# Delta rule of a hybrid layer: inverses' copies on ScalarE, fillers ahead of the first inverse, the third group's masks by adding transfers

## The chip, the cores and the metric

One core of a Trainium2 chip. The time is that of the device, in microseconds (us), from one launch; it is given as the median of several runs. Beside it stands one execution that the hardware profiler took. The engines are TensorE (PE: matmuls; PEld: its weight loads), VectorE (DVE), ScalarE (ACT), GpSimd (POOL) and SyncE (SP), which here only issues transfers. Each engine works off its own queue in order.

## The reference

One layer over 512 latent tokens and 256 context tokens, width 1024: half-step SwiGLU, then neighbourhood attention and a bidirectional gated delta rule (4 heads of 128) side by side, merged by sigmoid gates, then a second SwiGLU. The change is in the delta rule and at one place of the second SwiGLU. The delta rule in chunks, for keys k, values v, log decay g (summed inside the chunk) and beta:

```
decay = exp(where(lower, g[..., :, None] - g[..., None, :], -inf))
m     = where(strict, (k * beta) @ k.T * decay, 0)
u, w  = solve(I + m, [v * beta, k * beta * exp(g)])     # unit lower triangular
step:   v_new = u - w @ s
        o     = (q * exp(g)) @ s + (q @ k.T * decay) @ v_new
        s     = s * exp(g_last) + (k * exp(g_last - g)).T @ v_new
```

It runs forward and backward in time, first over the context, then over the latent tokens with the state that the context left.

## The kernel before, in words

All matmuls are in f32 split into a high and a low part (`split`, L137 on ACT and L139 on DVE), three products for one. Weights come through a stream (`Stream`): a transfer to `wr` (L175), a cast to `wh`, a difference `wl`. A weight can be queued behind instructions named in `behind`: the cast on ACT behind the first, the difference on DVE behind the second. For the second SwiGLU that table is `ws.behind` (L1654); `norms[t]` holds, for token tile t, the instruction that makes the normalized y (L130 on ACT) and the one that makes its bias nb (L129 on DVE).

The delta rule works on chunks of 128 tokens. There are six steps s = 0 to 5, in three groups of two (`bi` = 0, 1, 2), which makes four scans in a group, and for each step two pairs of heads p, each with two directions: four 128x128 matrices per (p, s).

`gram(p, s)` makes the decay matrix Dt and the two products. SP broadcasts a row of summed decays to all partitions (L1124); four DVE instructions subtract the partition's own sum and add the mask (L1128); ACT takes the exponential (L1129). Then Bt = products x beta x Dt (L1134, DVE), which goes out to DRAM (`bd`, L1137), and At for the outputs (L1140). `decay_place` says which buffer Dt has: the two buffers of tag `Dt` for s=0 and 1 with p=0 and for s=3, 4 and 5, parts of the output accumulators `oacc` for the rest.

`base_inverse` loads the 32x32 diagonal blocks of one group (L1158) into L, sets L's diagonal on POOL (L1161), and inverts them by 31 rows on DVE, each a product `bt` (L1165) and a sum `Xt` (L1166). It is a generator that stops after every fourth row. The result goes to DRAM (`rd`, L1169). L has one buffer, so a group's blocks can only be loaded when the rows of the group before are done.

`inverse` puts the blocks together to 128x128 inverses, two of them per group. It loads blocks (T<-rd, L1186), transposes them on DVE (L1188, L1189), copies them to T6 (L1199, ACT) and Tt (L1200, POOL), and then goes to and fro: small matmuls into `pi`, a copy Y to SBUF (L1208, DVE, 128x128), matmuls, negated copies (L1224 DVE, L1225 ACT), matmuls, a copy Y6 (L1235, DVE, 128x256; the profile writes Y for both), matmuls, a last negated copy into Tt (L1243, ACT).

`scan_step` is the recurrence: state times keys, `r` (L1266, DVE), inverse times r, `vn` (L1275, DVE), the scaled keys `ktail` (L1280, ACT), the new state (L1290, DVE), and for s >= 2 the outputs. After the last scan `gdn_out` normalizes them.

PE has few matmuls here and long waits between them, so other work is put between: the projections `FILLS`, 28 weight tiles of 8 k-slices, in quarters. One quarter (here: one step) is two slices with three 128x512 matmuls each. `turn(kind, i)` is called behind each group of small matmuls; it adds a rate from `RATE` to `due`, and issues as many whole steps as are due, behind the last matmul. Kind g stands in the products, l once before the first inverse, i in the inverses, s in the scans. Behind the last scan a loop (L1410) issues steps until all but the last `NLATE` tiles are done and a tile is complete; what is left follows with attention.

The order on each engine is made by a planner from program order and its own clock; `tc.issue_after(x)` forces an instruction behind x on the same engine. `marks` keeps the instructions for that. The program order of the delta rule is at its end: `grams` of a group, then `inv_of` (the inverses) and `scan_of`, with `step(base, n)` running n pieces of the base inverse of the group to come.

Of the kernel before, what the change touches and what calls it, by code (L numbers as in the profile page):

```python
# [12 lines left out]
AF = mybir.ActivationFunctionType  # L13
ALU = mybir.AluOpType
# [4 lines left out]
P = 128  # L19
# [39 lines left out]
def body(ctx, tc, I, out, dbg=None):  # L59
# [986 lines left out]
    spool, done = [gq], [0]  # L1046
    gb_, close_gb = pool("gbase", "right")
    FS, N0, NKQ, NLATE = 4, 2, 2, 3
    RATE = {"g": (2, 3.0, 0.7), "l": (7.2,), "i": (1.5, 0, 0), "s": (0.7, 0.9, 0.5)}
    NBT, NAT, NT6, NTT = 8, 8, 1, 2  # L1050

    last = [None]

# [59 lines left out]
    def decay_place(s, p):  # L1113

        if s == 2 or s < 2 and p == 1:
            a = 2 * (s == 2)
            return oaccs[p if s == 2 else s][:, a:a + 2].rearrange("p a b c -> p (a b) c")
        return tl(gb_, [P, 4, P], "Dt", 2)[:]

    def gram(p, s, bd, g):  # L1120

        mats = mats_of(s)
        Dt = decay_place(s, p)
        nc.sync.dma_start(Dt[:], bass.AP(gcd.tensor, gcd.offset + (4 * s + 2 * p) * P, [[0, P], [24 * P, 2], [1, 2 * P]]))  # L1124
        for m, (d, c, i) in enumerate(mats):
            msk = cst[:, (C_MF if d == 0 else C_MB):][:, 0:P]
            with tc.issue_after(marks["At" if s > 3 else "Bt"]) if s > 1 else nullcontext():
                V.scalar_tensor_tensor(Dt[:, m], Dt[:, m], gcum[:, d, s, 2 * p + i:2 * p + i + 1], msk, op0=ALU.subtract, op1=ALU.add)  # L1128
        S.activation(Dt[:], Dt[:], AF.Exp)  # L1129
        Bt, At = tl(gq, [P, 4, P], "Bt", NBT), None  # L1130
        for n, t in enumerate(products(p, s)):
            if n == 0:
                for m, (d, c, i) in enumerate(mats):
                    b = V.scalar_tensor_tensor(Bt[:, m], t[m] if s == 1 else t[:, m], beta[:, d, s, 2 * p + i:2 * p + i + 1], Dt[:, m], op0=ALU.mult, op1=ALU.mult)  # L1134
                if s < 2:
                    marks["Bt"] = b.ins
                nc.sync.dma_start(bass.AP(bd.tensor, bd.offset + g * MSTR, [[P, P], [4 * MSTR, 4], [1, P]]), Bt[:])  # L1137
            else:
                At = tl(gq, [P, 4, P], "At", NAT)
                a = V.tensor_tensor(At[:], t[:], Dt[:], ALU.mult)  # L1140
                if s < 4:
                    marks["At"] = a.ins
        return Bt, At


    def base_inverse(bd, rd):


        L = tl(gb_, [P, 32, 32], "L")
# [12 lines left out]
        for i in range(1, 32):  # L1162
            c = (i + 1) // 2
            t = tl(gb_, [P, 16, 32], "bt")
            V.tensor_tensor(t[:, 0:c, 0:i + 1], L[:, i:i + 1, 0:i + 1].to_broadcast([P, c, i + 1]), Xt[:, 0:c, 0:i + 1], ALU.mult)  # L1165
            V.tensor_reduce(Xt[:, 0:c, i], t[:, 0:c, 0:i + 1], AX, ALU.add, negate=True)  # L1166
            if i % 4 == 0:
                yield
# [10 lines left out]
    def inverse(bi, st, rd, Bts):  # L1179
# [16 lines left out]
        bt = lambda k, b: Bts[k % 2][:, k // 2 + (0 if b else 2)]  # L1196
        for b, r in enumerate(blk):
            o = 32 * (b % 2)
            S.copy(T6[r, :, o:o + 32], T0[r])  # L1199
            G.tensor_copy(Tt[r, :, 32 * b:32 * b + 32], T1[r])  # L1200
        py = tl(pgq, [P, 4, 32], "pi", 2)
        for k in range(4):
            for b, r in enumerate(blk):
# [1 line left out]
                mm(py[r, k, :], bt(k, b % 2)[q, r], T0[q, m, :], start=True, stop=True, tile_position=(32 * (b ^ 1), 32 * b))  # L1205
        turn("i", bi)
        Y = tl(gq, [P, 4, 32], "Y2", 2)
        V.tensor_copy(Y[:], py[:])  # L1208
        p0 = tl(pgq, [P, 4, 32], "pi", 2)
        p1 = tl(pgq, [P, 4, 32], "pi", 2)  # L1210
        for k in range(4):
# [20 lines left out]
                mm(py[hb[b], k, :], bt(k, b)[hb[1 - b], hb[b]], T6[hb[1 - b], m, :], start=True, stop=True, tile_position=(64 * (1 - b), 64 * b))  # L1232
        turn("i", bi)
        Y6 = tl(gq, [P, 4, 64], "Y6")
        V.tensor_copy(Y6[:], py[:])  # L1235
        p1 = tl(pgq, [P, 4, 64], "pi", 2)
        for k in range(4):
            for b in range(2):
# [1 line left out]
                mm(p1[hb[1 - b], k, :], Y6[hb[b], k, :], Tt[hb[b], m, hb[b]], start=True, stop=True, tile_position=(64 * b, 64 * (1 - b)))  # L1240
        turn("i", bi)
        for b in range(2):
            S.activation(Tt[hb[1 - b], sysm(b), hb[b]], p1[hb[1 - b]], AF.Copy, scale=-1.0)  # L1243
        return [[Tt[:, 4 * d + 2 * i + p] for d in range(2) for i in range(2)] for p in range(2)]

    def bc4(t, s, p):

        return t[:, :, s, 2 * p:2 * p + 2, None].to_broadcast([P, 2, 2, P])

    def v4(t):  # L1250
        return t.rearrange("p (d i) c -> p d i c", d=2)
# [3 lines left out]
    def scan_step(p, s, Tt, At, Sst):  # L1255
# [19 lines left out]
        V.tensor_tensor(v4(vn[:]), v4(pv[:]), bc4(beta, s, p), ALU.mult)  # L1275
# [57 lines left out]
    def grams(bi):  # L1333
        bd = tl(dp, [16 * MSTR], f"bd{bi}")[:]
        rds[bi] = tl(dp, [64, 1024], f"rd{bi}")[:]
        for j in (0, 2, 1, 3) if bi == 0 else range(4):
            res[(bi, j)] = gram(j % 2, 2 * bi + j // 2, bd, 2 * (j % 2) + j // 2)
        return base_inverse(bd, rds[bi])

    def step(gen, n=8):  # L1340
        for _ in range(n):
# [309 lines left out]
    ws = Stream(wp, [(w, key(j)) if key(j) else w for j, w in enumerate(src)], WB, 2)  # L1651
    ws.extra = {"b": (wb, 4, wp, WB), "c": (wc, 2, wp, WB)}

    ws.behind = {j: (norms[t]["y"], norms[u][m]) for j, t, u, m in ((2, 1, 2, "nb"), (3, 1, 2, "nb"), (4, 2, 3, "x2"), (5, 2, 3, "x2"), (6, 2, 3, "nb"), (7, 2, 3, "nb"))}  # L1654

    def h2(p, n):
        hs.append((tl(p, [P, NX], "hh", n, F32R), tl(p, [P, NX], "hl", n, F32R)))
# [280 lines left out]
```

## Time and profile before

| what | value |
|---|---|
| median of 3 runs | 1485.09 us (1483.22 to 1487.64) |
| the profiled execution's own time | 1482.26 us |
| its span, first to last instruction | 1480.5 us |
| mean granted TensorE clock | 0.995 of full speed |
| VectorE busy in the whole span | 77% |

How to read it: a page of the profile gives each engine's busy time; a list of waits names who waited for whom, with total, number and longest wait; a timeline row has the start in us, the duration, engine, line, operation, out<-in, shapes and count, and in brackets the idle time of the engine before it and what ended it; a row of a stretch gives its length, then for each engine the busy time and the number of instructions (PE, PEld, DVE, ACT, POOL), the granted clock, the share of the DMA engines and GB/s; a row of a group has its busy time, the mean of one in ns, and the idle time before.

### The profile page before, as it was taken

How to read it: one execution, taken by the hardware profiler on the slowest of the kernel's cores; microseconds unless marked ns; L12 is line 12 of the kernel's file. 1: busy time of each engine (PE TensorE's matmuls, PEld its weight loads, DVE VectorE, ACT ScalarE, POOL GpSimd, SP SyncE). 2: the span in 40 equal slices, each digit the busy share in tenths (PEclk: the TensorE clock that was granted, in tenths of full speed). 3: DMA queues.
4: the chain of work that ended last, by engine and by line, in shares of the span. 5: the costliest groups of instructions: out<-in, count | busy, mean ns of one | idle time of the engine just before them, and what ended most of it. 6: DMA issues, size and time to landing. Idle time of an engine off the chain costs nothing.

```text
span 1480.5 us, 23912 instructions
## 1 busy us (share of the span) xinstructions
PE 1430.8 (97%) x9117; PEld 1255.9 (85%) x9117; DVE 1144.0 (77%) x1975; ACT 661.7 (45%) x1090; POOL 214.6 (14%) x262
## 2 busy tenths in 40 slices
PE   6999999999999999999999899999999999999997
PEld 4789889999997777888877778877788999998886
DVE  8688869999987666768787885676668799886627
ACT  5435523434333387545544434376426454444310
POOL 1000000000000111223201001352321022220001
PEclk9999999999999999999999999999999999999999
DMA  9677764444569444222476523283344133234722
GB/s 377 206 250 250 240 232 172 162 161 165 164 212 400 181 160 150 79 93 94 153 227 209 163 68 126 93 302 108 120 157 171 38 129 114 94 106 144 257 99 85
DMA packets 109236, 248.56 MB, mean 168 GB/s; under 512 B 29049, under 2 KB 44481, under 8 KB 109121
## 3 DMA queue, kind: packets, MB, share of 16 engines
q1 hardware_dynamic: 104480, 229.40, 45.8%
q0 software_dynamic: 3056, 12.33, 2.2%
q10 hardware_dynamic: 1586, 5.32, 0.9%
q8 instruction: 71, 1.16, 0.3%
q14 instruction: 43, 0.35, 0.1%
HBM read 215.50 MB, written 31.50 MB: 167 GB/s over the span
## 4 chain that ended last, share of the span: by engine, by line
PE 72%; DVE 11%; DMA 8%; issue 3%; ACT 3%; POOL 2%; SPq 1%; DVEq 0%; POOLq 0%; ACTq 0%
PE ps L212 17%; PE ps L534 5%; PE ps L536 5%; PE ps L535 5%; PE pm L193 4%; PE pm L194 4%; PE pm L195 4%; PE ps L193 3%; PE ps L195 3%; PE ps L194 3%; PE ps L1712 3%; PE ps L1714 3%; PE ps L1713 3%; PE pc L1055 2%; DVE wl L139 2%
## 5 line engine op out<-in xcount | busy, mean ns | idle before, releaser
L137 ACT CAST wh<-wr 128x1024 fp32r<-128x1024 f32 (+1 forms) x184 | 185.4, 1013 | 270.6 <-PE pm L194 67.5
L139 DVE TENSOR_TENSOR wl<-wr,wh 128x1024 fp32r<-128x1024 f32 (+1 forms) x184 | 225.1, 1228 | 102.2 <-ACT wh L137 101.8
L193 PE MATMUL pm<-uxh,wh 128*128 128x512 f32 x320 | 131.3, 410 | 0.2
L195 PE MATMUL pm<-uxh,wl 128*128 128x512 f32 x320 | 126.3, 395 | 1.0 <-DVE wl L139 1.0
L194 PE MATMUL pm<-uxl,wh 128*128 128x512 f32 x320 | 126.0, 394 | 0.0
L212 PE MATMUL ps<-wh,hx 128*128 128x512 f32 x352 | 96.3, 391 | 1.1 <-ACT wh L137 1.1
L212 PEld LDWEIGHTS ps<-wh,hx 128*128 128x128 f32 x352 | 65.9, 188 | 15.7 <-ACT wh L137 1.9
L281 DVE SCALAR_TENSOR_TENSOR adap<-wr,crow 128x1024 f32<-128x1024 f32 x61 | 74.3, 1218 | 0.7 <-ACT crow L289 0.3
L195 PEld LDWEIGHTS pm<-uxh,wl 128*128 128x128 f32 x320 | 60.5, 189 | 14.2 <-DVE wl L139 1.2
L114 POOL TENSOR_TENSOR rs<-ve,mhalf 128x1 f32<-128x1 f32 (+2 forms) x46 | 50.3, 1095 | 141.5 <-DVE ve L110 139.1
L193 PEld LDWEIGHTS pm<-uxh,wh 128*128 128x128 f32 x320 | 60.7, 190 | 11.3 <-ACT u L152 0.4
L194 PEld LDWEIGHTS pm<-uxl,wh 128*128 128x128 f32 x320 | 60.7, 190 | 10.4
L193 PE MATMUL ps<-uh,wh 128*128 128x256 f32 (+1 forms) x208 | 68.2, 328 | 0.4 <-ACT wh L137 0.4
L194 PE MATMUL ps<-ul,wh 128*128 128x256 f32 (+1 forms) x208 | 67.3, 324 | 0.0
L195 PE MATMUL ps<-uh,wl 128*128 128x256 f32 (+1 forms) x208 | 67.1, 325 | 0.0
L194 PE MATMUL ps<-uxl,wh 128*128 128x256 f32 (+1 forms) x192 | 60.5, 317 | 0.8 <-DVE uxl L139 0.8
L137 ACT CAST wh<-ra 128x1024 fp32r<-128x1024 f32 x31 | 32.6, 1052 | 62.1 <-PE ps L535 20.2
L195 PE MATMUL ps<-uxh,wl 128*128 128x256 f32 (+1 forms) x192 | 60.2, 317 | 0.0
L193 PE MATMUL ps<-uxh,wh 128*128 128x256 f32 (+1 forms) x192 | 59.7, 317 | 0.0
L534 PE MATMUL ps<-ur,wh 128*128 128x384 f32 x168 | 56.5, 336 | 0.0
L535 PE MATMUL ps<-ur,wh 128*128 128x384 f32 x168 | 56.4, 336 | 0.0
L534 PE MATMUL ps<-uh,wh 128*128 128x384 f32 x168 | 56.4, 336 | 0.0
(502 smaller groups left out, 4246.8 us busy)
## 6 DMA issues: line engine op xcount, KB each, us to landing
wr<-in_w_adaT_dram SPq DMA_DIRECT2D x64, 512.0 KB, 4.6
wr<-in_up_dram SPq DMA_DIRECT2D x56, 512.0 KB, 3.4
wr<-in_win_dram SPq DMA_DIRECT2D x52, 512.0 KB, 3.4
wr<-in_dn_dram SPq DMA_DIRECT2D x51, 512.0 KB, 3.7
ra<-in_up_dram SPq DMA_DIRECT2D x24, 512.0 KB, 4.3
rb<-in_up_dram SPq DMA_DIRECT2D x18, 512.0 KB, 3.3
ra<-in_w_adaT_dram SPq DMA_DIRECT2D x16, 512.0 KB, 4.5
wr<-in_w_o_dram SPq DMA_DIRECT2D x8, 512.0 KB, 4.3
```

The lines of the kernel that those rows point to most:

```text
L114: G.tensor_tensor(rs[:], ve[:], mhalf[:, 0:n], ALU.pow)
L137: marks["hi"] = S.copy(hi, src).ins
L139: marks["lo"] = V.tensor_tensor(lo, src, hi.bitcast(F32), ALU.subtract).ins
L193: T.matmul(ps, a, uh[:, k, :], start=(k == 0), stop=False)
L194: T.matmul(ps, a, ul[:, k, :], start=False, stop=False)
L195: marks["mm"] = T.matmul(ps, b, uh[:, k, :], start=False, stop=(k == nk - 1)).ins
L212: T.matmul(banks[t][d][:, c0:c1], a[:, sl], b[:, d * 512 + c0:d * 512 + c1], start=first and j == 0, stop=last and j == 2)
L281: V.scalar_tensor_tensor(pr[:], raw[:], 1.0, crow, op0=ALU.mult, op1=ALU.mult, accum_out=col[:, c:c + 1])
L534: T.matmul(ps[:], a, mh, start=k == 0, stop=False)
L535: T.matmul(ps[:], a, ml, start=False, stop=False)
L536: T.matmul(ps[:], b, mh, start=False, stop=k == 3)
L1712: T.matmul(ps[:], a, uh[:, k], start=k == 0, stop=False)
```

## The change

- The rate l goes from 7.2 to 10.2: three more steps ahead of the first inverse.
- Y and Y6 are copied by ACT in place of DVE.
- For s = 4 and 5, SP loads the mask into Dt from a new DRAM input, GpSimd issues a transfer that adds the broadcast row to it, and ACT takes four exponentials (128x128) with the negated sums `ngc` as bias. The adding transfers for s = 5 are queued behind the last Tt copy on POOL; the exponentials behind the last T6 copy (s = 4) or the last negated Tt copy (s = 5) traced so far.
- Dt of s = 3 has a buffer of the scans' tag `r`.
- The first row of the third base inverse is queued on DVE behind `vn` of the latest scan, and the first four pieces of that inverse are traced after the first group's fourth scan.
- In the second SwiGLU the cast of weight 7 is queued behind y of token tile 3 in place of tile 2.

```diff
-    RATE = {"g": (2, 3.0, 0.7), "l": (7.2,), "i": (1.5, 0, 0), "s": (0.7, 0.9, 0.5)}
+    RATE = {"g": (2, 3.0, 0.7), "l": (10.2,), "i": (1.5, 0, 0), "s": (0.7, 0.9, 0.5)}
+    ngc = tl(gq, [P, 2, 2, 4], "ngc")
+    S.activation(ngc[:], gcum[:, :, 4:6], AF.Copy, scale=-1.0)
...
+        if s == 3:
+            return tl(gq, [P, 4, P], "r", 2)[:]
         return tl(gb_, [P, 4, P], "Dt", 2)[:]
...
+        if s > 3:
+            nc.sync.dma_start(Dt[:], I["msk"])
+            with tc.issue_after(marks["Tt"]) if s > 4 else nullcontext():
+                G.dma_start(Dt[:], row, accum_op=ALU.add)
+            with tc.issue_after(marks["Ti" if s > 4 else "T6"]):
+                for m, (d, c, i) in enumerate(mats):
+                    S.activation(Dt[:, m], Dt[:, m], AF.Exp, bias=ngc[:, d, s - 4, 2 * p + i:2 * p + i + 1])
+        else:
+            nc.sync.dma_start(Dt[:], row)
...
+            with tc.issue_after(marks["vn"]) if late and i == 1 else nullcontext():
+                V.tensor_tensor(t[:, 0:c, 0:i + 1], L[:, i:i + 1, 0:i + 1].to_broadcast([P, c, i + 1]), Xt[:, 0:c, 0:i + 1], ALU.mult)
...
-        V.tensor_copy(Y[:], py[:])
+        S.copy(Y[:], py[:])
...
-        V.tensor_copy(Y6[:], py[:])
+        S.copy(Y6[:], py[:])
...
     scan_of(0, 2)
-    step(base, 2)
     scan_of(0, 3)
-    step(base, 2)
+    step(base, 4)
     inv_of(1, 0)
...
-    ws.behind = {j: (norms[t]["y"], norms[u][m]) for j, t, u, m in (..., (6, 2, 3, "nb"), (7, 2, 3, "nb"))}
+    ws.behind = {j: (norms[t]["y"], norms[u][m]) for j, t, u, m in (..., (6, 2, 3, "nb"), (7, 3, 3, "nb"))}
```

More of the change, by code (lines that the diff above doesn't have):

```diff
@@ L1123, in gram @@
         Dt = decay_place(s, p)
[L1124 to L1129, printed above, removed]
+        row = bass.AP(gcd.tensor, gcd.offset + (4 * s + 2 * p) * P, [[0, P], [24 * P, 2], [1, 2 * P]])
+        if s > 3:
[7 more added lines that the diff above has]
+            nc.sync.dma_start(Dt[:], row)
+            for m, (d, c, i) in enumerate(mats):
+                msk = cst[:, (C_MF if d == 0 else C_MB):][:, 0:P]
+                with tc.issue_after(marks["Bt"]) if s > 1 else nullcontext():
+                    V.scalar_tensor_tensor(Dt[:, m], Dt[:, m], gcum[:, d, s, 2 * p + i:2 * p + i + 1], msk, op0=ALU.subtract, op1=ALU.add)
+            S.activation(Dt[:], Dt[:], AF.Exp)
         Bt, At = tl(gq, [P, 4, P], "Bt", NBT), None
@@ L1143, in gram, with base_inverse @@
         return Bt, At
-    def base_inverse(bd, rd):
+    def base_inverse(bd, rd, late):
         L = tl(gb_, [P, 32, 32], "L")
@@ L1164, in base_inverse @@
             t = tl(gb_, [P, 16, 32], "bt")
-            V.tensor_tensor(t[:, 0:c, 0:i + 1], L[:, i:i + 1, 0:i + 1].to_broadcast([P, c, i + 1]), Xt[:, 0:c, 0:i + 1], ALU.mult)
+            with tc.issue_after(marks["vn"]) if late and i == 1 else nullcontext():
+                V.tensor_tensor(t[:, 0:c, 0:i + 1], L[:, i:i + 1, 0:i + 1].to_broadcast([P, c, i + 1]), Xt[:, 0:c, 0:i + 1], ALU.mult)
             V.tensor_reduce(Xt[:, 0:c, i], t[:, 0:c, 0:i + 1], AX, ALU.add, negate=True)
@@ L1198, in inverse @@
             o = 32 * (b % 2)
-            S.copy(T6[r, :, o:o + 32], T0[r])
-            G.tensor_copy(Tt[r, :, 32 * b:32 * b + 32], T1[r])
+            marks["T6"] = S.copy(T6[r, :, o:o + 32], T0[r]).ins
+            marks["Tt"] = G.tensor_copy(Tt[r, :, 32 * b:32 * b + 32], T1[r]).ins
         py = tl(pgq, [P, 4, 32], "pi", 2)
@@ L1242, in inverse @@
         for b in range(2):
-            S.activation(Tt[hb[1 - b], sysm(b), hb[b]], p1[hb[1 - b]], AF.Copy, scale=-1.0)
+            marks["Ti"] = S.activation(Tt[hb[1 - b], sysm(b), hb[b]], p1[hb[1 - b]], AF.Copy, scale=-1.0).ins
         return [[Tt[:, 4 * d + 2 * i + p] for d in range(2) for i in range(2)] for p in range(2)]
@@ L1274, in scan_step @@
         vn = tl(gq, [P, 4, P], "vn", 2)
-        V.tensor_tensor(v4(vn[:]), v4(pv[:]), bc4(beta, s, p), ALU.mult)
+        marks["vn"] = V.tensor_tensor(v4(vn[:]), v4(pv[:]), bc4(beta, s, p), ALU.mult).ins
         Sn = None
@@ L1337, in grams @@
             res[(bi, j)] = gram(j % 2, 2 * bi + j // 2, bd, 2 * (j % 2) + j // 2)
-        return base_inverse(bd, rds[bi])
+        return base_inverse(bd, rds[bi], bi == 2)
     def step(gen, n=8):
@@ L1652, in body @@
     ws.extra = {"b": (wb, 4, wp, WB), "c": (wc, 2, wp, WB)}
-    ws.behind = {j: (norms[t]["y"], norms[u][m]) for j, t, u, m in ((2, 1, 2, "nb"), (3, 1, 2, "nb"), (4, 2, 3, "x2"), (5, 2, 3, "x2"), (6, 2, 3, "nb"), (7, 2, 3, "nb"))}
+    ws.behind = {j: (norms[t]["y"], norms[u][m]) for j, t, u, m in ((2, 1, 2, "nb"), (3, 1, 2, "nb"), (4, 2, 3, "x2"), (5, 2, 3, "x2"), (6, 2, 3, "nb"), (7, 3, 3, "nb"))}
     def h2(p, n):
@@ L1892, in layout @@
     a["cst"] = _consts()
+    a["msk"] = np.repeat(a["cst"][:, C_MF:C_MF + 2 * P].reshape(P, 2, 1, P), 2, 2).reshape(P, 4, P)
     a["rope"] = _rope()
```

## The prediction

> **What bounds the kernel now.** I read the page's head first, then TensorE's list of waits for 705 to 965 us (the delta rule and the start of attention), then the timeline around each wait, and last the granted clock in the throttle's own steps.
>
> ```profile
> span 1480.5 us, 23912 instructions
> PE 1430.8 (97%) x9117; PEld 1255.9 (85%) x9117; DVE 1144.0 (77%) x1975; ACT 661.7 (45%) x1090; POOL 214.6 (14%) x262
> ```
>
> TensorE (PE) is the bound: 97% busy. Nothing in the change takes matmuls away, so whatever it gains is PE's idle time, 1480.5 - 1430.8 = 49.7 us in the whole span, and in the delta rule only these waits matter:
>
> ```profile
> PE pi L1055 <- DVE Y L1235: 4.0, 2, 2.4
> PE pi L1055 <- DMA T<-rd: 3.4, 1, 3.4
> PE pc L1055 <- DVE bt L1165: 2.6, 1, 2.6
> ```
>
> The reader is to see that each of the three has an edit aimed at it: the Y copies move to ScalarE (ACT), fillers are put ahead of the first inverse (T<-rd is the inverse's input), and a row of the third base inverse (bt) goes behind a scan. Where they stand:
>
> ```profile
> 794.26 0.56 PE L1055 MATMUL pi<-T,Bt 32*32 32x32 f32 x32 [3.43 <-DMA T<-rd]
> ...
> 825.62 0.68 PE L1055 MATMUL pi<-Tt,Y 64*64 64x64 f32 x16 [2.37 <-DVE Y L1235]
> ...
> 846.86 1.13 PE L1055 MATMUL pc<-vn,ktail 128*128 128x128 f32 x8 [2.60 <-DVE bt L1165]
> ...
> 862.01 0.68 PE L1055 MATMUL pi<-Tt,Y 64*64 64x64 f32 x16 [1.60 <-DVE Y L1235]
> ...
> 902.14 0.45 PE L1055 MATMUL pi<-T,Bt 32*32 32x32 f32 x32
> ```
>
> Two of these waits cost more than themselves. In the stretches below the column after the engines' busy times is the granted clock:
>
> ```profile
> 791.04:794.45 3.41, 0.19 (x23) 0.22 (x27) 2.67 (x8) 0.53 (x2) 0.00 (x1) 1.00 0.79 216
> 794.45:797.87 3.42, 3.42 (x57) 2.32 (x49) 2.08 (x11) 1.93 (x5) 1.57 (x4) 0.50 0.67 184
> 859.31:862.72 3.41, 1.39 (x41) 1.24 (x45) 3.21 (x12) 1.61 (x4) 0.00 (x0) 1.00 0.00 0
> 862.72:866.13 3.41, 3.11 (x42) 2.88 (x43) 2.20 (x7) 0.76 (x2) 0.00 (x0) 0.50 0.02 5
> ```
>
> After a stretch of 3.41 us in which PE was busy 0.19 or 1.39 us, the next one ran at half clock: 3.41 x 0.5 = 1.7 us of matmul work lost each time, while PE looks busy.
>
> **The change part by part.** I call one call of the filler generator a step.
>
> *A, three more fillers.* The matmuls of one step are six of 512 columns:
>
> ```profile
> 960.25 0.50 PE L193 MATMUL pm<-uxh,wh 128*128 128x512 f32 x1
> ...
> 961.05 0.40 PE L193 MATMUL pm<-uxh,wh 128*128 128x512 f32 x1
> ...
> 962.44 0.39 PE L193 MATMUL pm<-uxh,wh 128*128 128x512 f32 x1
> ...
> 964.94 1.03 PE L1469 MATMUL pt<-ident,pr 128*128 128x128 f32 x8
> ```
>
> From 961.05 to 962.44 there are six starts, so a step is 1.39 us and three are 4.2. They fill the 3.43 us before 794.26 and make the inverse start about 0.7 later, which is work moved and no loss. The code's rates show whence they come: all turns give 93.8 steps beside the 8 at the start, so 101 are done, and the closing loop rounds up to 104, three more. With 10.2 for 7.2 the turns reach 104 and the loop adds none. So three floating steps leave the end of the delta rule. Gain: 3.43 and the clock's 1.7, together 5.1. Given back: the cover at the end. From 960.25 to 964.94 fillers stand between attention's scores and its first transposes, which really wait for
>
> ```profile
> 960.28 1.22 DVE L1458 TENSOR_REDUCE nm<-sc 128x2 f32<-128x1024 f32 x1
> ```
> ```profile
> 962.26 0.68 ACT L1462 ACTIVATE pr<-sc,nm 128x512 f32<-128x512 f32 x1
> ```
>
> that is until about 962.9. If all 4.2 us are missing here, 4.69 - 4.2 = 0.5 of cover stays, and 962.9 - 960.25 - 0.5 = 2.2 us become idle; if they are missing from elsewhere, nothing. I take the middle, 1.1. A = +4.0 (2.9 to 5.1).
>
> *B, Y copies on ACT.* They leave DVE and cost ACT about the same, by its nearest PSUM copies:
>
> ```profile
> L1235 DVE COPY Y<-pi 128x256 f32<-128x256 f32 x6 | 2.5, 420 | 1.2 <-PE pi L1055 1.2
> ...
> L1208 DVE COPY Y<-pi 128x128 f32<-128x128 f32 x6 | 1.7, 276 | 0.0
> ```
> ```profile
> L1243 ACT ACTIVATE Tt<-pi 64x256 f32<-64x256 f32 x12 | 4.5, 378 | 10.3 <-PE pi L1055 10.3
> ```
>
> Twelve copies at up to 0.38 are at most 4.6 us on an engine that is 45% busy; 4.2 us leave DVE. What matters is the queue each copy stands in:
>
> ```profile
> 821.98 0.63 ACT L1129 ACTIVATE Dt<-Dt 128x512 f32<-128x512 f32 x1 [3.85 <-DVE Dt L1128]
> ...
> 826.34 0.77 ACT L1243 ACTIVATE Tt<-pi 64x256 f32<-64x256 f32 x2 [1.01 <-PE pi L1055]
> ...
> 860.46 1.64 ACT L1199 COPY T<-T 32x256 f32<-32x256 f32 x4 [1.72 <-issue]
> ```
>
> Before 821.98 ACT sat idle 3.85 us, so the wait of 2.37 goes whole. At 860.46 four copies of the next inverse may stand ahead, 1.64 us, as long as the wait of 1.60: I take half, 0.8. With the idle time the half clock at 862.72 should mostly go: 1.2 of 1.7. B = +4.4 (0.8, if two such queues remain, to 5.7). The stretch from 859.31, in which PE was busy 1.39 us, was no idle one, and half clock followed all the same. The Trainium skill, "TensorE: Matmul & The Clock Gate", Part 1: The HAM clock gate, has the clock halved after at least one idle window of about 3.4 us; the trace disagrees, and by that rule the second loss would have another cause and stay, B 3.2 and the sum 6.6.
>
> *C, first row of the third base inverse behind a scan.*
>
> ```profile
> 845.38 0.16 DVE L1165 TENSOR_TENSOR bt<-L,Xt 128x2 f32<-128x2 f32 x1 [2.24 <-POOL L L1161]
> ...
> 846.04 0.68 DVE L1275 TENSOR_TENSOR vn<-pc,beta 128x512 f32<-128x512 f32 x1
> ...
> 853.48 0.69 DVE L1275 TENSOR_TENSOR vn<-pc,beta 128x512 f32<-128x512 f32 x1
> ...
> 890.35 0.68 DVE L1166 TENSOR_REDUCE Xt<-bt 128x16 f32<-128x512 f32 x1
> ```
>
> The row held DVE until its data came, and vn, on which PE waited 2.60 us, stood behind it. With the row behind the vn of 853.48 (the first group's fourth scan) this wait goes: C = +2.6 (0 if vn finds another blocker, to 2.6). The added wait delays the 31 rows, which end at 890.35; priced under E.
>
> *D, masks of the third group.* Off DVE: 16 masks, here the eight of the window 790 to 930.
>
> ```profile
> L1128 DVE SCALAR_TENSOR_TENSOR Dt<-Dt,gcum,cst 128x128 f32<-128x128 f32 x8 | 2.3, 345 | 2.4 <-DMA Dt<-gcd 2.4
> ```
> ```profile
> L1280 ACT ACTIVATE ktail<-ktok,etg 128x128 f32<-128x128 f32 x36 | 11.5, 390 | 13.4 <-PE pc L1055 13.4
> ```
>
> DVE loses 16 x 0.345 = 5.5 us; ACT gets 16 x 0.39 for four of 0.63, +3.7 us. SP's queue keeps four transfers (now the mask), and POOL's gets four adding ones, behind Tt copies. No trace shows an adding transfer; its bounds are SP's row broadcast and the slowest one that POOL issues:
>
> ```profile
> Dt<-gcd SPq DMA_DIRECT2D x8, 256.0 KB, 5.2
> ...
> xr<-x1d POOLq DMA_DIRECT2D x4, 512.0 KB, 6.1
> ```
>
> I reckon with the slower, 6.1. PE waits for no mask, and the last exponentials are queued behind the Tt copies of 826.34 (to 827.1), long enough to hide the extra transfer: D = 0 (0.9 gain, the share of DVE's queue, to 8 us loss: 6.1 and 1.9 for exponentials, if nothing hides them). The second group's masks for s=3 only move to a buffer that the scans use later, and the negated sums are one small ACT operation: 0.
>
> *E, the wait that comes instead.* By 902.14, where PE enters the third group's inverses, it has earned 1.7 - 0.7 + 4.4 + 2.6 = 8.0 us. Those inverses need the rows, and DVE has little room:
>
> ```profile
> 854.20:891.00 36.80, 34.41 (x392) 28.86 (x391) 32.51 (x92) 13.34 (x34) 2.26 (x6) 0.95 0.16 55
> ```
>
> DVE is busy 32.51 of 36.80 us. The rows that ran before 854 must go in here (an estimate of some 17 instructions, the first of 0.16, 2.9 us in all), and about three of the twelve Y copies leave (1.1); so 890.35 can come forward by 0 to 2.5 us, not by 8. The rest, 5.5 to 8, is covered only as far as PE does what is left of the second group's last scan first. E = -4.5 (0 to -8).
>
> *F, cast of weight 7 behind the last y.*
>
> ```profile
> 1140.09 1.05 ACT L137 CAST wh<-wr 128x1024 fp32r<-128x1024 f32 x1 [0.66 <-DMA wr<-in_up_dram]
> 1141.04 1.24 ACT L130 ACTIVATE y<-xr,nb,rs 128x1024 f32<-128x1024 f32 x1
> ```
> ```profile
> 1139.47 0.21 DVE L129 TENSOR_SCALAR nb<-bmv,rs 128x1 f32<-128x1 f32 x1
> ```
> ```profile
> 1142.33 1.09 PE L148 MATMUL ps<-ident,y 128*128 128x128 f32 x8 [1.64 <-ACT y L130]
> ```
>
> y is ready to run at 1139.7 and starts at 1141.04: 1.3 us earlier, of PE's 1.64. The cast that falls behind feeds the last product of this round, over 2 us later. F = +1.3 (0 to 1.6).
>
> **Sum.** 4.0 + 4.4 + 2.6 + 0 - 4.5 + 1.3 = 7.8 us. The profiled execution took 1482.26 us (span 1480.5 and 1.8 around it); the median of the runs is 1485.09, 2.8 above it. I take the saving off the median: 1477.3.
>
> **The rivals.**
> 1. *Given back at the third group.* E at its full 8.0 and A at 2.9: 2.9 + 4.4 + 2.6 + 1.3 - 8.0 = 3.2 us, 1481.9. For it: DVE's 32.51 of 36.80, and rows started 8 us later. Against: PE has a scan left to do.
> 2. *The third group comes later than before.* Place: mask transfer, adding transfer, exponentials, Bt, rows, one after the other. Price: 6.1 + 1.9 = 8 us on top of rival 1, 1489.9. It decides once the first inverse of the group starts about 8 us after 902.14. Against: the hiding under D.
> 3. *The order isn't what the words say.* Engine orders come from a planner's clock; if the three steps land elsewhere, A is 0: 3.8 us, 1481.3.
> 4. *POOL is held by DVE while it issues the adding transfers.* Its copies show such a delay:
>
> ```profile
> L1200 POOL COPY Tt<-T x24: 386/393/1447, 794.6 to 906.5; 32x256 f32<-32x256 f32 x24
> ```
>
> 1447 for a usual 393 is 1.05 us; two transfers in a row, 2.1 on top of rival 1: 1484.0. The Trainium skill has the rule ("SBUF — State Buffer", section SBUF: two separate sides): descriptors of POOL's transfers are starved while DVE holds the shared port. No row of this case shows a starved transfer.
>
> **How the numbers follow.** Forecast 0.62 (its own range 1470.5 to 1481), rival 1 0.17, rival 2 0.09, rival 3 0.07, rival 4 0.05. A measurement of this kernel tells 0.3%, 4.5 us, from no change: faster is below 1480.6, slower above 1489.5. Faster: nearly all of the forecast (0.59) and the low edges of rivals 1 and 3 (0.02), 0.61; slower: rival 2, 0.09; same: the rest, 0.30. The range: the low end is E near 0 with A, B and F near their upper bounds, rounded in a little (5.1 + 5.7 + 2.6 + 1.6 = 15.0, 1470.1); the high end, 1486.5, holds rivals 1, 3 and 4 with their spread and leaves out rival 2.
>
> **What would show it.** Right: no wait over 1 us for T<-rd near 794 and clock 1.00 after it; no PE wait for Y from DVE, short ones from ACT; no vn behind bt near 846; PE waiting a few us for T<-rd or for short hops at the third group's inverses; y's wait near 1142 under 0.5. Wrong: a first inverse of the third group more than 3 us later than 902, over 2.5 us of idle PE at attention's start, or Y copies on ACT behind weight casts.

## The result and the profile after

The changed kernel takes 1495.84 us in the median (six runs, 1493.44 to 1496.93), the kernel before 1484.31 in the same comparison (six runs, 1479.68 to 1487.64). The ratio is 1.0079 (95% interval 1.0067 to 1.0091): 0.8%, some 11.7 us, slower. The forecast was 1477.3, and faster. The head of the page of after:

```profile
span 1494.0 us, 23911 instructions
PE 1439.3 (96%) x9117; PEld 1261.1 (84%) x9117; DVE 1138.8 (76%) x1947; ACT 667.2 (45%) x1115; POOL 220.5 (15%) x266
```

The same 9117 matmuls keep PE busy 8.5 us longer than before (1430.8), and its idle time went from 49.7 to 54.7 us. PE's list of waits from 705 to 975 us (total, number, longest):

```profile
PE pi L1057 <- DMA T<-rd: 4.2, 2, 3.3
...
PE pi L1057 <- DVE T L1238: 2.9, 3, 1.1
PE pc L1057 <- DVE r L1280: 2.5, 2, 2.0
...
PE pm L193 <- ACT spill L801: 2.0, 1, 2.0
PE pi L1057 <- ACT Y L1222: 1.7, 1, 1.7
```

T<-rd is still on it, although most of its wait at the old place is gone. PE's timeline shows where the waits stand now:

```profile
794.28 0.21 PE L1057 MATMUL pi<-T,Bt 32*32 32x32 f32 x2 [0.98 <-DMA T<-rd]
...
848.38 1.23 PE L1057 MATMUL pc<-r,Tt 128*128 128x128 f32 x4 [2.01 <-DVE r L1280]
...
916.96 0.65 PE L1057 MATMUL pi<-T,Bt 32*32 32x32 f32 x32 [3.25 <-DMA T<-rd]
919.33 0.59 PE L1057 MATMUL pi<-Y,T 32*32 32x32 f32 x21 [1.72 <-ACT Y L1222]
...
972.19 0.80 PE L193 MATMUL pm<-uxh,wh 128*128 128x512 f32 x1 [2.01 <-ACT spill L801]
...
1155.15 1.09 PE L148 MATMUL ps<-ident,y 128*128 128x128 f32 x8 [0.32 <-ACT y L130]
```

The reader is to see that the aimed-at waits did go: 3.43 near 794 is 0.98, no Y from DVE is left, 1.64 for y is 0.32. But the third group's first inverse, at 902.14 before, starts at 916.96, and with nothing left to interleave. The clock, by its own steps, with the step behind the old first wait on top:

```profile
794.28:797.70 3.42, 3.42 (x44) 2.58 (x45) 2.49 (x11) 3.35 (x7) 1.57 (x4) 1.00 0.87 263
848.40:855.23 6.83, 6.69 (x88) 5.65 (x89) 3.44 (x12) 3.69 (x8) 0.16 (x1) 0.50 0.61 160
916.67:930.32 13.65, 9.29 (x241) 8.38 (x241) 4.03 (x13) 7.57 (x24) 3.14 (x8) 0.50 0.24 67
967.87:978.11 10.24, 8.23 (x38) 6.67 (x35) 4.90 (x8) 3.90 (x11) 2.38 (x4) 0.50 0.78 247
```

That is 30.7 us at half clock, against 6.8 before. DVE's timeline at the third base inverse's first and last row:

```profile
860.73 0.68 DVE L1289 TENSOR_TENSOR vn<-pc,beta 128x512 f32<-128x512 f32 x1
861.33 0.20 DVE L1179 TENSOR_TENSOR bt<-L,Xt 128x2 f32<-128x2 f32 x1
...
906.22 0.69 DVE L1180 TENSOR_REDUCE Xt<-bt 128x16 f32<-128x512 f32 x1
```

The row stands behind vn, as asked. It stood at 845.38 before, and the last sum at 890.35: both came 16 us later. In sum the first scores of attention start 8.9 us later, counted from each run's first transfer Dt<-gcd (711.4 and 711.5 us), they last 5.5 us longer, and y gives 1.3 back: 13.1 of the 13.5 us between the spans.

The longer scores are in part an earlier start. The last scan's product of state and queries (S,qT) and the first scores, in the kernel before and in the changed one:

```profile
942.23 1.06 PE L1055 MATMUL pc<-S,qT 128*128 128x128 f32 x8
...
958.52 0.39 PE L1454 MATMUL sc<-kah,qah 64*128 64x256 f32 x2
```
```profile
954.35 1.06 PE L1057 MATMUL pc<-S,qT 128*128 128x128 f32 x8
...
967.51 0.39 PE L1467 MATMUL sc<-kah,qah 64*128 64x256 f32 x2
```

Between the two rows PE has 48 filler matmuls before and 30 now, three steps fewer, so the scores follow 3.1 us sooner. S,qT itself comes 12.1 us later, and from it to the end of the scores it is 93.9 us before and 96.3 now. So most of the loss, 12.1 us, is made ahead of the last scan's S,qT, and 2.4 behind it.

### The profile page after: what moved, and what is told of

The parts are those of the page before. It is cut to its first block, busy times and chain, and to the rows that moved or that the text cites. A ratio compares the mean times of both kernels' runs of the same rounds, so it can differ in the third digit from the quotient of the medians.

```text
span 1494.0 us, 23911 instructions
## 1 busy us (share of the span) xinstructions
PE 1439.3 (96%) x9117; PEld 1261.1 (84%) x9117; DVE 1138.8 (76%) x1947; ACT 667.2 (45%) x1115; POOL 220.5 (15%) x266
## 4 chain that ended last, share of the span: by engine, by line
PE 66%; DVE 15%; DMA 8%; issue 4%; ACT 4%; POOL 2%; SPq 1%; DVEq 0%; ACTq 0%; POOLq 0%
PE ps L212 15%; PE ps L534 4%; PE ps L536 4%; PE ps L535 4%; PE pm L193 4%; PE pm L194 4%; PE pm L195 4%; PE ps L193 3%; PE ps L195 3%; PE ps L194 3%; PE pc L1057 3%; DVE wl L139 2%; PE ps L1725 2%; PE ps L1727 2%; PE ps L1726 2%
## 5 line engine op out<-in xcount | busy, mean ns | idle before, releaser
L137 ACT CAST wh<-wr 128x1024 fp32r<-128x1024 f32 (+1 forms) x184 | 185.5, 1013 | 254.7 <-PE pm L194 56.2
L193 PE MATMUL pm<-uxh,wh 128*128 128x512 f32 x320 | 132.2, 413 | 2.0 <-ACT spill L801 2.0
L114 POOL TENSOR_TENSOR rs<-ve,mhalf 128x1 f32<-128x1 f32 (+2 forms) x46 | 50.1, 1090 | 137.3 <-DVE ve L110 135.0
```

Source lines behind the costliest of these rows:

```text
L114: G.tensor_tensor(rs[:], ve[:], mhalf[:, 0:n], ALU.pow)
L137: marks["hi"] = S.copy(hi, src).ins
L193: T.matmul(ps, a, uh[:, k, :], start=(k == 0), stop=False)
```

## The experiments

The question was which part brings the delay. Theory R: the forced row. Theory M: the masks by adding transfers (rival 2's chain). Theory F: the three steps that are missing behind the last scan. Theory H came later: the third group's first inverse sets the end, whatever delays it. Eighteen kernels were run. The table has all of them; times are counted from each run's own first transfer Dt<-gcd (709.5 to 714.2 us), columns: start of the third base inverse's first row, of the third group's first inverse, of attention's first score matmul, length of the scores (first to last), time from the last scan's S,qT to the end of the scores, ratio to before. The times are those of one execution of each kernel, which lay up to 3.8 us from the kernel's median; the ratio is that of all its runs. "Base" is before with B, F and the row behind the third scan's vn.

| kernel | row | inverse | scores from | scores last | S,qT to end | ratio (95%) |
|---|---|---|---|---|---|---|
| before | 134.0 | 190.7 | 247.1 | 77.6 | 93.9 | 1 |
| changed | 149.8 | 205.5 | 256.0 | 83.1 | 96.3 | 1.0079 (1.0067–1.0091) |
| changed, row and order as before | 139.0 | 200.5 | 253.3 | 84.0 | 97.2 | 1.0050 (1.0030–1.0069) |
| changed, masks on DVE | 147.1 | 204.2 | 254.7 | 83.4 | 96.5 | 1.0091 (1.0076–1.0106) |
| changed, l 7.2 | 146.9 | 202.8 | 256.3 | 79.2 | 95.5 | 1.0045 (1.0030–1.0059) |
| changed, Y on DVE | 153.4 | 209.0 | 257.9 | 81.3 | 94.5 | 1.0052 (1.0036–1.0068) |
| before + B + F | 130.9 | 187.0 | 245.3 | 80.7 | 97.0 | 0.9971 (0.9958–0.9984) |
| base | 133.2 | 187.7 | 244.3 | 78.5 | 94.8 | 0.9960 (0.9947–0.9973) |
| before + A | 136.8 | 194.0 | 251.7 | 84.0 | 97.3 | 1.0086 (1.0068–1.0104) |
| before + C | 143.6 | 198.3 | 251.6 | 79.1 | 95.5 | 1.0048 (1.0031–1.0066) |
| base + A | 140.4 | 201.4 | 251.6 | 84.0 | 97.1 | 1.0049 (1.0029–1.0068) |
| base + A, steps from the start | 134.6 | 194.4 | 249.3 | 79.5 | 95.8 | 1.0002 (0.9989–1.0016) |
| changed, four more at the end | 150.7 | 207.6 | 263.9 | 81.4 | 94.8 | 1.0111 (1.0089–1.0133) |
| base + D | 137.3 | 197.7 | 251.2 | 79.2 | 95.5 | 1.0030 (1.0020–1.0040) |
| base, none added at the end | 132.2 | 186.6 | 244.4 | 81.4 | 93.9 | 0.9980 (0.9965–0.9994) |
| base + A, steps from the scans | 138.1 | 198.9 | 250.9 | 81.0 | 97.3 | 1.0006 (0.9996–1.0016) |
| base, one step | 138.2 | 194.7 | 253.0 | 81.0 | 96.3 | 1.0035 (1.0021–1.0048) |
| base, thinner fillers | 131.8 | 186.3 | 239.4 | 90.0 | 105.5 | 1.0011 (0.9999–1.0024) |
| changed, output buffers | 150.4 | 206.2 | 257.0 | 81.7 | 94.9 | 1.0087 (1.0069–1.0106) |
| base, output buffers | 133.0 | 187.2 | 243.8 | 78.1 | 94.4 | 0.9960 (0.9947–0.9972) |

A difference of 0.001 is 1.5 us. Two ratios less than 0.002 apart are not told apart here.

### The change with one part undone

**The row.**

```diff
-        return base_inverse(bd, rds[bi], bi == 2)
+        return base_inverse(bd, rds[bi], False)
...
     scan_of(0, 2)
+    step(base, 2)
     scan_of(0, 3)
-    step(base, 4)
+    step(base, 2)
```

> The changed kernel with the third base inverse's first row no longer queued behind a scan's vn, and its first four pieces again traced as two and two around the first group's fourth scan. Theory R (the forced row is the cause: in the changed kernel L was there at 851, the first row ran at 861.33, behind the vn of 860.73, and the third group's first inverse began at 917.0, against 902.1 before): the first row runs at about 851, the first inverse at about 907, half clock after it is gone, and the time falls by 7 to 10 us, to 1486 to 1489. Theory M (the masks and exponentials came late, so L at 851 and not 845 is what counts): the row runs at 851 here too, but the gain is under 5 us. Theory F (three fillers fewer behind the last scans): the time stays within 2 us of 1495.8.

1.0050: 4 us below the changed kernel, less than R asked. DVE's and then PE's timeline of this kernel say why:

```profile
849.52 0.16 DVE L1179 TENSOR_TENSOR bt<-L,Xt 128x2 f32<-128x2 f32 x1 [5.34 <-POOL L L1174]
```
```profile
851.44 1.65 PE L1057 MATMUL pc<-r,Tt 128*128 128x128 f32 x6 [4.89 <-DVE r L1280]
```

Free of the scan, the row is queued before its data and holds DVE 5.34 us; r stands behind it, and PE waits 4.89. The rows ran earlier, and the stop came back, some twice as long as before. R's 7 to 10 us and its inverse near 907 are missed (it starts at 911.0); what M said of this run came true.

**The masks.** The branch `if s > 3` is taken out, s = 3 has its old buffer.

> The changed kernel with the masks of s=4 and 5 subtracted on DVE again, and Dt of s=3 in its old buffer; all else as changed. Theory M: L is loaded at about 845 again, the rows start earlier, the time falls by 6 to 10 us. Theory R: the row still waits for the vn at about 861, the first inverse of the third group stays at 915 to 918, and the time stays within 3 us of 1495.8. Theory F: no more than 2 us either way.

1.0091, not told apart from 1.0079. The row still waits for vn (147.1 in the table). So inside the whole change the masks cost nothing: theory M falls as the cause there.

**The steps.** `"l": (7.2,)`.

> The changed kernel with the rate l at 7.2 again, so that the three steps run behind the last scan. Theory F (what is given back at the end: three steps of cover gone, the clock halved at 967.87 for 10.24 us, 5.1 us lost there, and 2.01 and 1.36 us of idle PE): the time falls by 3 to 7 us in spite of the wait near 794 that returns. Theories R and M: the wait of 3.4 us near 794 and its half clock return, so does the cover at the end; the sum is between 2 us faster and 5 us slower than 1495.8.

1.0045, 5 us faster; the scores last 79.2 for 83.1, and no half clock stands at their start. The time is what theory F asked for, the place is not: the last scan's S,qT starts 3.0 us sooner than in the changed kernel, and from it to the end of the scores it is only 0.8 us less (95.5 for 96.3).

**The Y copies.** `V.tensor_copy` in both places.

> The changed kernel with Y and Y6 copied by DVE again. If the copies on ACT bring what the prediction gave them (4.4 us), the time rises by 3 to 5 us. If the third group's inverses are exposed to ACT's longer way (waits of 1.72 and 0.98 us for Y from ACT at 919.33 and 923.61 at half clock), the time falls by 1 to 3 us.

1.0052, 4 us faster, more than the 1 to 3 expected, while the same copies on ACT made the kernel before faster (next run). A part's worth depends on what stands around it; which wait makes the difference here is not shown.

### One part alone

**B and F**, and then with `base_inverse`'s first row behind the latest vn, but the pieces traced as before, so that it is the third scan's (this is the base).

> The kernel before with only the Y and Y6 copies on ACT and the cast of weight 7 behind the last y (parts B and F of the prediction). If B and F are worth what the prediction gave them, 4.4 + 1.3: 5 to 6 us faster than before, no PE wait over 1.2 us for Y6 near 825 and 862. If the copies on ACT only move the wait to another queue (undoing B alone made the changed kernel 4 us faster), F stays and the time is within 2.5 us of before.

> As the run with B and F alone, and the first row of the third base inverse behind the vn of the first group's third scan (846.0 in before), not the fourth: program order as before. Theory R (the row was queued one scan too far): vn no longer waits 2.24 us behind the row, the rows start about 1 us later than before, the third group's first inverse stays within 2 us of 902, and the time falls by 2 to 3 us below the run without it. Theory that any row behind a scan costs: the time is no lower than the run without it.

0.9971 and 0.9960: 4.3 us faster (2.4 to 6.2 by the interval), and 5.9 with the row. B and F are worth about what was predicted. The row's own 1.6 us are not told apart from nothing, but queued one scan earlier than in the change it costs nothing, which speaks for R. The base beats both kernels.

**A alone.** `"l": (10.2,)`.

> The kernel before with the rate l at 10.2 alone (part A). By the prediction: 4.0 us faster (2.9 to 5.1). By theory F (the three steps are missed behind the last scan, where the clock halves): the wait near 794 goes, half clock of 7 us or more comes at attention's start, and the time is the same to 4 us slower than before.

1.0086: 12.8 us slower, more than the whole change. It is both worse than predicted and worse than theory F. PE's timeline, then DVE's:

```profile
804.55 0.55 PE L1055 MATMUL pi<-Y,T 32*32 32x32 f32 x32 [3.63 <-DVE Y L1208]
...
853.67 2.08 PE L1055 MATMUL pc<-r,Tt 128*128 128x128 f32 x8 [4.31 <-DVE r L1266]
```
```profile
850.97 0.16 DVE L1165 TENSOR_TENSOR bt<-L,Xt 128x2 f32<-128x2 f32 x1 [4.62 <-POOL L L1161]
```

No wait is left near 794, but Y, then still on DVE, now stands behind a weight's wl and a transpose, 3.63 us; and the third group's first row waits 4.62 us for L ahead of r. The last scan's S,qT starts 7.5 us later than before, and from it to the end of the scores it is 3.4 us more.

**C alone.**

> The kernel before with part C alone: the first row of the third base inverse behind the vn of the first group's fourth scan, four pieces traced there. By the prediction C earns 2.6 and the rows are late by up to as much: -2.6 to +5 us against before. Theory R: the row starts at about 854 and not 845, the rows end some 8 us later than 890.4, the third group's first inverse begins at 908 to 911 after a wait of PE for T<-rd of 2 us or more with half clock behind it, and the time is 3 to 8 us above before.

1.0048: 7.1 us slower (4.6 to 9.8). The row starts 9.6 us later than before and the inverse 7.6. DVE (third column after the length) in the stretch ahead of the forced row and the one behind it, first in this kernel:

```profile
846.40:856.00 9.60, 8.72 (x83) 7.50 (x82) 5.76 (x17) 4.32 (x10) 1.03 (x4) 1.00 0.43 123
856.00:900.00 44.00, 40.40 (x425) 33.55 (x425) 39.00 (x116) 15.02 (x38) 2.28 (x6) 0.96 0.19 67
```

and then in the kernel before, behind its first row:

```profile
845.40:854.20 8.80, 7.34 (x72) 6.37 (x73) 7.96 (x33) 4.32 (x10) 0.93 (x3) 1.00 0.35 85
```

Before, rows filled DVE's gaps in those 8.8 us (0.8 us idle). With the row held back DVE idles 3.8 of 9.6 us, and behind it is as full as ever: the 31 rows move as a block. R holds for C alone.

### Parts on the base, and the order

**A on the base**, and A with the three steps taken from the eight at the start (`range(N0 * FS - 3)`).

> B, F and the row behind the third scan's vn (the run with ratio 0.996), plus part A: l at 10.2. If A's steps are good once the Y copies are on ACT and only the DVE order spoilt them in the run of A alone: 2 to 5 us faster than that run, ratio 0.993 to 0.995. Theory F (three steps of cover are missed behind the last scan and the clock halves at attention's start): the wait near 794 and its half clock go, attention's scores last 4 to 6 us longer, and the time is 2 to 6 us slower than that run, ratio 0.997 to 1.000.

> As the run of B, F, row and A, but the three steps are taken from the eight ahead of the first products, so that three again run behind the last scan. Theory F: attention's scores are as short as without A (77 to 80 us), and the time is 3 to 6 us below the run with A; unless the start of the delta rule, near 700 to 735, now waits instead, which its waits would show. If the end is not what counts: within 2 us of the run with A.

A costs 13 us here too (1.0049 against 0.9960), so it isn't only the Y copy's queue on DVE. Of them 10.5 us are lost up to the last scan's S,qT and 2.3 behind it. With three steps fewer at the start 7 of the 13 us come back, 5.5 of them ahead of S,qT and 1.3 behind it. The work ahead of the first inverse is then what it was in the base, PE's wait there is back (2.74 us), and yet the third group's inverse stays 6.7 us late.

**More cover at the end.** `NLATE` 1 in the changed kernel.

> The changed kernel with four more steps behind the last scan, taken from those that follow in attention's first head (NLATE 1 in place of 3). Theory F: the half clock of 10.24 us at attention's start goes, the time falls by 3 to 6 us, to about 1490. If attention's first head misses them there, it gives back some 2 to 4 us, and the time stays within 2 us of 1495.8.

1.0111: the half clock of 10.24 us is down to two steps of 3.41, and the time rose by 4.7 us. The four steps are taken from attention's first head, where PE now waits 2.21 us for pr and 2.22 for vw. So moving them doesn't cure it; what more cover would do without taking it from there is not shown.

**D on the base.**

> The run of B, F and the row behind the third scan's vn, plus part D (adding transfers, exponentials on ACT). If D costs nothing, as the prediction had it: ratio 0.995 to 0.997. If the chain of mask transfer, adding transfer, exponentials, Bt and rows is late wherever the row doesn't hide it (L was there at 851 with D, at 840 without it in the changed kernel): the first row moves from 843.6 to 849 or later, vn or r waits 2 to 5 us behind it on DVE, and the time is 4 to 9 us above that run.

1.0030 against 0.9960: 10 us slower, a little over the upper figure of the second expectation. Timelines of DVE, ACT and PE:

```profile
849.51 0.16 DVE L1179 TENSOR_TENSOR bt<-L,Xt 128x2 f32<-128x2 f32 x1 [3.34 <-POOL L L1174]
```
```profile
847.13 1.92 ACT L1172 COPY L<-Ltr 64x1024 f32<-64x1024 f32 x1 [2.25 <-DMA Ltr<-bd]
848.86 0.29 ACT L1222 COPY Y<-pi 128x128 f32<-128x128 f32 x1
```
```profile
849.21 0.59 PE L1057 MATMUL pi<-Y,T 32*32 32x32 f32 x21 [3.50 <-ACT Y L1222]
```

L comes late, as theory M has it: POOL sets its diagonal at 849.3, in the base at 841.5. And the late copy into L stands ahead of a Y copy on ACT, which is B's doing: PE waits 3.50 us. Rival 2's chain is real; in the whole change the forced row, later still, hides it.

**Why so much for three steps?** Four kernels were added. One has the rate 0.667 for 0.5 in the third group's scans; one has A with 0.4 for 0.7 in the first group's scans; one has l at 8.2, a single step; one leaves out the middle of the three products in three of the fillers' tiles, so that these outputs are less exact:

```diff
+        if not thin:
+            T.matmul(ps, a, ul[:, k, :], start=False, stop=False)
...
+            for _ in fill_spill(spool[0], n, m, dst[n], FS, 23 <= j < 26):
```

> B, F and the row behind the third scan's vn (ratio 0.996, third group's first inverse at 898.1), plus a rate of 0.667 for 0.5 in the third group's scans: three steps more there, so that none is added behind the last scan, as with A, but nothing is put ahead of the first inverse. Theory F (A's cost is the missing cover at the end): attention's scores last 81 to 84 us for 78.2, the time is 4 to 6 us above that run, ratio 0.9990 to 1.0005. Theory H (what counts is when the third group's first inverse starts; from it to the end of attention's scores it was 132 to 134 us in most kernels so far): the first inverse stays at 898 and the time within 2 us of that run, ratio 0.995 to 0.9975.

> The same base plus l at 10.2 with the first group's scans at 0.4 for 0.7, so that the three steps ahead of the first inverse come from the scans behind it and not from the end. Theory H with A's work as the delay: by the third group's rows as many steps have run as without A, the first inverse comes back to 898 to 901, the wait near 794 goes and stays gone, the time is 0 to 4 us below the base, ratio 0.993 to 0.996. If it is not the amount of work but where the planner puts the later orders: the first inverse at 905 or later, the time 5 us or more above the base.

> The same base with l at 8.2: one step more ahead of the first inverse, one fewer behind the last scan. If A's cost (13.9 us for three steps) grows with the steps: 4 to 5 us above the base, ratio 0.9985 to 0.9995. If it comes from orders that flip at some point: within 2 us of the base, or the whole 10 us and more at once.

> The same base, but the fillers' tiles 23 to 25 (steps 92 to 103, all behind the third group's first inverse) leave out the middle one of their three products, so these outputs have less than full precision: 24 matmuls of 0.23 us fewer, 5.5 us of PE's work. If PE is the bound from the third group's first inverse on: 4 to 5.5 us below the base, ratio 0.9925 to 0.9935. Theory H with a dependent chain as the bound there: the end of attention's scores and the time fall by less than 2 us, ratio 0.9945 or more.

*None added at the end*: 0.9980, inverse at 186.6, scores 81.4. Moving three steps from the end into the scans costs about 3 us, between the two expectations, and not surely told apart from the base. *Steps from the scans*: 1.0006, 7 us above the base, inverse 11.2 us late: the amount of work done by then isn't it. *One step*: 1.0035, 11 us for 1.4 us of work. The cost doesn't grow with the steps; it comes at once, and the order shows how. PE in the base and then with one step, without the fillers:

```profile
841.89 1.05 PE L1055 MATMUL pc<-r,Tt 128*128 128x128 f32 x8
...
843.81 1.13 PE L1055 MATMUL pc<-vn,ktail 128*128 128x128 f32 x8 [0.87 <-DVE bt L1166]
...
846.17 1.05 PE L1055 MATMUL pc<-S,kT 128*128 128x128 f32 x8
...
848.53 0.43 PE L1055 MATMUL pi<-T,Bt 32*32 32x32 f32 x26
```
```profile
843.84 1.05 PE L1055 MATMUL pc<-r,Tt 128*128 128x128 f32 x8
...
848.29 0.65 PE L1055 MATMUL pi<-T,Bt 32*32 32x32 f32 x32 [3.40 <-DMA T<-rd]
848.87 2.08 PE L1055 MATMUL pc<-vn,ktail 128*128 128x128 f32 x8
```

In the base (and before) the second group's first inverse stands behind the third scan's vn,ktail and S,kT, and behind fillers. With one step more it stands ahead of vn,ktail, its blocks aren't there, and the scan waits behind it. The same turn, with the inverse ahead of the third scan's r or vn products, stands in the base with A (2.00 us for T<-rd), with A from the start (3.34), with A from the scans (4.47), with D (1.73), and in the changed kernel (at 845.94, with r 2.01 us late behind it). The changed kernel with l 7.2 has it too, so undoing A does not undo it where D is in:

```profile
840.75 0.39 PE L1057 MATMUL pi<-T,Bt 32*32 32x32 f32 x24 [1.65 <-DMA T<-rd]
841.34 1.26 PE L1057 MATMUL pc<-r,Tt 128*128 128x128 f32 x8 [0.20 <-DVE r L1280]
```

Before with A alone doesn't have it; there the two waits quoted above stand in its place. On the base the first rows go with the turn: 134.6 to 140.4 with it, 131.8 to 133.2 without. That the planner makes it because its own clock has PE later is argued, not shown, and a kernel with A and that order forced back was not tried: the last link of A's cost stays open.

*Thinner fillers*: 24 matmuls, 5.5 us of PE's work, are missing behind the third group's first inverse, and the time rose by 7.6 us against the base. The scores start 4.9 us sooner and last 11.5 us longer. PE's timeline:

```profile
955.11 0.50 PE L193 MATMUL pm<-uxh,wh 128*128 128x512 f32 x1 [2.44 <-ACT spill L802]
...
975.57 0.69 PE L1484 MATMUL po<-pT,vw 128*64 128x128 f32 x2 [5.54 <-ACT pT L1473]
```

So in this kernel PE's work is not what bounds the end of the delta rule and attention's start; less of it brought waits and 10.2 us of half clock. Both expectations missed.

Theory H does not hold as it stands. From the third group's first inverse to the end of the scores the table has 130 to 143 us, and three kernels with that inverse at 194.0, 194.4 and 194.7 have the ratios 1.0086, 1.0002 and 1.0035. From the last scan's S,qT to the end of the scores it is 93.9 to 97.3 us in nineteen of the twenty kernels; the thinner fillers, with 105.5, are the exception. Nine of the nineteen are three steps short ahead of the scores (30 filler matmuls) and nine are not (48); both groups have the same range. So the end of the scores follows the last S,qT, and the missing cover behind it (theory F) shows no cost of its own beyond that spread of 3.4 us.

**The output buffers.** In the changed kernel ACT shows, ahead of the spill that PE waits for at 972.19:

```profile
970.97 0.69 ACT L1341 ACTIVATE vn<-pc,nw 128x512 f32<-128x512 f32 x1 [3.05 <-DMA obd<-vn]
971.55 0.58 ACT L801 COPY spill<-pm 128x512 f32<-128x512 f32 x1
```

```diff
-            o = tl(gq, [P, 4, P], "vn", 2)[:].rearrange("p t c -> p (t c)")
+            o = tl(gq, [P, 4, P], "r" if p else "vn", 2)[:].rearrange("p t c -> p (t c)")
```

> The changed kernel with the last two of the four staged outputs (vn<-pc) in the two buffers of tag r, which are free by then, in place of the two of tag vn. Theory S (attention's start gives back because four outputs in a row share two buffers: in the changed kernel ACT waits 3.05 us at 970.97 for obd<-vn, the spill queued behind it comes at 971.55, PE waits 2.01 us for it at 972.19 and the clock is halved from 967.87 to 978.11): that wait of ACT goes, PE's 2.01 goes, at most 3.4 us of half clock stay, and the time falls by 3 to 6 us, to 1490 to 1493. If the missing cover is the cause and not the buffers: the wait moves to another engine and the time stays within 2 us of 1495.8.

> The fastest kernel so far (B, F, row behind the third scan's vn; ratio 0.996) with the same buffers for the last outputs. There ACT waited for no obd<-vn and attention's scores lasted 78.2 us, so by theory S nothing is to be had: ratio 0.9945 to 0.9975.

In the changed kernel with this edit ACT's, then PE's timeline:

```profile
966.98 1.27 ACT L1341 ACTIVATE r<-pc,nw 128x512 f32<-128x512 f32 x2 [1.90 <-PE pc L1060]
968.14 0.59 ACT L801 COPY spill<-pm 128x512 f32<-128x512 f32 x1
```
```profile
981.19 0.66 PE L1495 MATMUL po<-pT,vw 128*64 128x128 f32 x8 [2.96 <-DVE vw L1451]
```

The spill comes 2.2 us sooner (counted from each run's start), the wait of 2.01 us is gone, and 6.8 us of half clock too. The scores are 1.4 us shorter, and the time (1.0087) is not told apart from the changed kernel's. A wait of 2.96 us for vw came instead. Theory S falls: its 3 to 6 us are not there. On the base the edit does nothing, as expected. So the scores last 3 to 6 us longer where three steps have left the end mostly because they start some 3 us sooner behind the last scan. What is left of it, 2.3 to 3.4 us with A alone, on the base and in the whole change, lies inside the spread of S,qT to the end, and its cause is not settled.

## Why the prediction was wrong, step by step

- **A, +4.0.** The local half was right: 0.98 us left of 3.43, full clock behind it. Measured alone it is -12.8 us on before and -13 on the base. The step that failed is "make the inverse start about 0.7 later, which is work moved and no loss": it held all orders behind that point fixed. On the base one step more was enough to turn the second group's inverse and the third scan round on PE; on the kernel before other waits came, 3.63 us for Y and 4.31 for r. The last scan's S,qT starts 7.5 us later on the kernel before and 10.5 on the base. The second term, a give-back of 0 to 2.2 at attention's start, was near in size (2.3 to 3.4 us from S,qT to the end of the scores) and wrong in place: between the first scores and the first transposes, where it was reckoned, 19 of 20 filler matmuls stayed; what went were 18 of the 48 ahead of the scores.
- **B, +4.4, and F, +1.3.** Together 4.3 us measured for 5.7, inside B's range. No wait for Y6 over 1.2 us was left at the second group's inverses, and y's wait fell from 1.64 to 0.32. Of ACT's queue the four copies of the next inverse were priced and weight casts named as a sign; the copy into L (1.92 us) was not seen, and behind it PE waited 3.50 us with D.
- **C, +2.6, with E, -4.5.** Alone together -7.1 us for -1.9. In that run PE's wait near 846 did fall, from 2.60 to 0.88. The step that failed is E's "the rows that ran before 854 must go in here (an estimate of some 17 instructions, the first of 0.16, 2.9 us in all)", and its result, that the end of the rows "can come forward by 0 to 2.5 us". The row of DVE's load (32.51 of 36.80 us) was read rightly as no room, but then 2.9 us were let in and 1.1 taken out. In fact DVE idled 3.8 us ahead of the row with C alone; in the changed kernel the row came at 861.3, behind a vn of 860.7 and not of 853.5 (the scan it is tied to moves as well), and the end of the rows went back by 16 us.
- **D, 0.** Right in the whole change (1.0091 without it, 1.0079 with it), wrong as a reason: the queue of Tt copies doesn't hide the chain, the later row does. Alone on the base it costs 10 us, above the upper bound of 8 that was named. The transfer's price was near its bounds of 5.2 and 6.1: 4.6 to 5.8 us in the changed kernel, though 6.3 to 7.0 in the run with Y on DVE. The 1.9 us for exponentials come out of no row: four of 0.39 are 1.6.
- **The rivals.** Rival 2 had the place: it was to decide once the inverse starts 8 us after 902, and it starts 14.8 after. Its chain was there (D on the base) but was not what came last. Rival 1 had the right row of the profile and too small a price. Rival 3 named the planner's order, but let it take only A's gain away, not what lies behind. Rival 4: the issue of each adding transfer took 1.2 to 1.3 us on POOL, for 1.05 in the rival, but only ACT waited for one of them, 2.28 us, and no PE wait stands behind that; whether DVE had a part in the 1.2 is not shown.
- **The sum.** Measured one by one (D on the base), A, C with E, D, and B with F make +12.8 + 7.1 + 10 - 4.3 = some 26 us; together 11.7. Terms were added that all delay the last scan. That the latest of them hides the others is shown for the masks behind the row; how the 12.1 us ahead of S,qT divide among the parts is open, as no part undone alone gives back more than some 5.

## What to carry to other kernels

Where a planner lays out the orders of all engines, an edit far ahead can turn round two instructions behind it: price the order after the edit, not the old order with a piece moved, and test one step before three. An instruction that an in-order engine reaches before its data holds up what stands behind it. Tying it behind the nearest such work cost nothing here, and gained nothing that can be told apart; a scan further the whole chain behind it moved, for 7 us. And edits that touch one chain do not add: measure each alone and undo each from the whole before any is kept; here B, F and the row one scan earlier are 0.4% faster than before, and the rest of the change ate that and more.

## What the runs showed of the hardware

The clock halves without an idle step. The three steps of 3.41 us ahead of the half clocks of the changed kernel, PE's busy time first behind the length:

```profile
844.99:848.40 3.41, 1.40 (x32) 0.83 (x30) 1.56 (x3) 2.27 (x4) 1.18 (x3) 1.00 1.08 239
913.25:916.67 3.42, 0.46 (x2) 0.02 (x1) 1.59 (x3) 2.09 (x4) 3.16 (x3) 1.00 0.90 273
964.45:967.87 3.42, 1.58 (x14) 1.20 (x16) 1.63 (x3) 1.40 (x3) 1.39 (x2) 1.00 0.22 81
```

PE was busy 1.40, 0.46 and 1.58 us of 3.41. From 700 to 1100 us of all twenty traces, every full-clock step with less than 1.45 us busy was followed by half clock, none with more than 2.2, and between the two it went either way. By the Trainium skill, "TensorE: Matmul & The Clock Gate", Part 1: The HAM clock gate, it takes an idle window of about 3.4 us; the traces agree on the length and not on idle: a step that is two fifths busy is enough. And less half clock is not less time by itself: with the output buffers 6.8 us of it went, a wait of 2.96 us came, and the time stayed.

The adding transfers, 256 KB each, by the view of their line in the changed kernel:

```profile
L1132 POOL DMA_DIRECT2D Dt<-gcd x4: 1195/1222/1307, 740.0 to 826.6; - x4
...
DMA to landing us min/median/max: 4.6/5.5/5.8
```

The times to landing are about those of SP's plain row broadcasts in the kernel before (median 5.2), and the issue takes 1.2 to 1.3 us of POOL. With Y on DVE the same four took 6.3 to 7.0 us; why is not shown.
